# Two more down rounds per layer by seven block products, and the weight sums of the gate and up units made by accumulating transfers

## The chip, the cores and the metric

The kernel runs on one core of a Trainium2 chip. The metric is the device time of one execution in microseconds, from runs without the profiler. The profile is of one other execution of the same program; it names the engines PE (matrix multiplication; PEld is its weight load), DVE (vector engine), ACT (scalar engine), POOL (GpSimd) and SP (the engine whose queue issues most transfers).

## The reference

Two decoder layers over 528 positions (16 learned meta tokens, then 512 tokens) with 1024 features. Each layer has a norm, an input projection, forgetting attention and retention heads side by side, an output projection, and then the part that is changed here, a gated feed-forward network of 2816 hidden features:

```
hn = rmsnorm(h, ffn_norm_g)
ff = silu(hn @ w_gate) * (hn @ w_up)      # 528 x 1024 by 1024 x 2816, twice
h  = h + ff @ w_down                      # 528 x 2816 by 2816 x 1024
```

All inputs and outputs are float32. In the second layer only the 512 real tokens are needed after the attention, since the meta tokens are dropped at the end.

## The kernel before

Features lie on the 128 partitions and tokens in the free dimension, so `h` is eight tiles of 128x528. A float32 product is made of three fast ones: each operand is split into a rounded part "hi" (written by ACT) and the rest "lo" (subtracted by DVE), and PE adds hi*hi, hi*lo and lo*hi. So each block of 128x128 weights costs three matmuls per stretch of tokens, and each weight has to be converted by ACT and DVE first (`splits`, lines L941 and L942).

The feed-forward part goes over 22 hidden tiles f of 128 features. Tiles 0 and 1 are made plainly. Each tile from 2 on is a *unit* (class `Unit`): gate and up for that f, over two halves of the input features and two halves of the tokens, are a 2x2 by 2x2 block product, and are made by seven block products instead of eight (the Strassen-Winograd scheme). That is 7 x 4 blocks x 3 = 84 matmuls of 264 tokens (256 in layer 1) instead of 96, for which sums of weights and of inputs are needed. The weight sums were made by DVE, four additions of 128x512 per unit: L1084, L1085 (`make2`), L1092 (`make3`) and L1098 (`make4`). The sums of the inputs (`x_forms`) are made once per layer, in tiles `th`/`tl`.

The down projection is done in *rounds* of hidden tiles, `ROUNDS = ((0, 2), (2, 6), (6, 10), (10, 14), (14, 18), (18, 22))`, numbered 0 to 5. A round's products are woven between those of the following round's units: each of its four units brings one pair p of output tiles (2p, 2p+1). A plain pair costs 8 weight blocks x 3 x 528 tokens: 48 matmuls of 264 in layer 0, and in layer 1 24 of 512. For rounds in `SEVENTHS` (before: 2 and 4) the pair (class `Pair`) is again a 2x2 by 2x2 block product in seven: 7 x 2 blocks x 3 = 42 matmuls of 264 (256). For it, each pair needs sums of the down weights (`make1`, `make2`, four DVE additions of 128x256, L1012, L1013, L1018, L1020) and each round needs four sums of activations, the *token forms* (`token_forms`), made by DVE and split by ACT and DVE. Form 1 is made in the third-last and fourth-last unit of its round, forms 2, 3 and 4 in the last two. Forms 2 and 3 lie in parts of the tiles `xh`/`xl` of the input (its second token half, which the units don't read in that form), and form 4 in `sqh`/`sql`, one buffer each.

Results gather in PSUM tiles: `psa` (four banks, x and keep) and `psd` (two pairs of banks); DVE adds them to `h` (L1041, L1039) or takes them into the activation (L1124 to L1139), and only then PE can use the bank again.

What sets the order: PE's instructions stand in the order that the program writes them. Those of ACT, DVE, POOL and SP are put in order by a scheduler, with priorities and a few pinned places; each engine then works off its own queue strictly in that order, and an instruction that waits holds up all behind it. Weight transfers are issued by SP (L1072 gate and up, L1006 and L1177 down) into rings: `raw` with four buffers of 512 KB, `fraw` with two. Converted weights lie in two rings, `whi`/`wlo` with two buffers and `fwhi`/`fwlo` with three. `need(j)` starts conversions three to five weight jobs ahead of their use. In the feed-forward part POOL does nothing.

## Time and profile before

| | |
|---|---|
| time, three runs | 1249.72, 1249.9 and 1250.13 us (median 1249.9) |
| the profiled execution | span 1248.2 us from the first to the last instruction; the page gives no time of its own around it, and the median lies 1.7 us above the span |
| PE busy | 1236.6 us (99%), 9387 matmuls |
| DVE busy | 1062.2 us (85%), 2033 instructions |
| ACT busy | 733.5 us (59%) |
| POOL busy | 294.6 us (24%), none of it in the feed-forward parts |
| transfers | 116.25 MB, 93 GB/s over the span |
| feed-forward part | from about 282 to 634 us (layer 0) and from about 887 to 1232 us (layer 1) |

Times in the profile are counted from the span's start. Busy time overlaps between engines. Matmuls are pipelined, so the duration of one in the profile (280 ns) is longer than the distance from one to the next; the chain of waits, which merges runs of matmuls with their count, gives that distance.

### The profile page before, as it was taken

The numbers are of one execution on the slowest core, as the hardware profiler recorded it, in microseconds if no ns is written. First come the engines' busy times: TensorE is split into PE (matmuls) and PEld (weight loads), VectorE is DVE, ScalarE is ACT, GpSimd is POOL, SyncE is SP. The second block draws the span as 40 slices with busy tenths as digits, with TensorE's granted clock in tenths as the row PEclk, the third lists the DMA queues.
The fourth block names the chain that finished last, engine by engine and source line by source line (L and its number), as shares of the span: only waits on it lengthen the run. The fifth ranks groups of instructions, "written<-read, shape, count | busy, mean of one in ns | idle before, by whom it ended". The sixth has DMA issues, their size and how long they took to land.

```text
span 1248.2 us, 24164 instructions
## 1 busy us (share of the span) xinstructions
PE 1236.6 (99%) x9387; PEld 1192.1 (96%) x9387; DVE 1062.2 (85%) x2033; ACT 733.5 (59%) x1397; POOL 294.6 (24%) x568
## 2 busy tenths in 40 slices
PE   9999999999999999999999999999999999999997
PEld 9999999999999999999999989999799999999996
DVE  7887756889997999899876877568999989998996
ACT  7767655776544555455566766567765445454554
POOL 4555655440000000000035556554400000000000
PEclk9999999999999999999999999999999999999999
DMA  6222222222433233322312222231414333333322
GB/s 238 68 77 69 78 69 85 60 85 72 133 119 102 85 102 118 103 86 85 114 65 85 63 84 75 68 94 52 141 54 135 111 102 102 100 104 102 102 69 69
DMA packets 43347, 116.25 MB, mean 93 GB/s; under 512 B 5088, under 2 KB 9952, under 8 KB 43232
## 3 DMA queue, kind: packets, MB, share of 16 engines
q1 hardware_dynamic: 42800, 114.41, 28.8%
q8 instruction: 74, 1.21, 0.4%
q14 instruction: 41, 0.34, 0.1%
q10 hardware_dynamic: 432, 0.29, 0.1%
HBM read 112.58 MB, written 2.10 MB: 92 GB/s over the span
## 4 chain that ended last, share of the span: by engine, by line
PE 90%; DVE 5%; ACT 2%; DMA 1%; issue 1%; SPq 0%; ACTq 0%; DVEq 0%
PE psd L231 28%; PE psa L953 22%; PE psd L953 15%; PE psd L1197 8%; PE psa L231 5%; PE psa L1197 3%; PE psa L452 2%; PE psa L619 2%; PE psa L549 1%; PE psa L753 1%; PE psa L789 1%; DMA raw<-w_down 1%; DVE wlo L942 1%; DVE fwlo L942 0%; PE psa L312 0%
## 5 line engine op out<-in xcount | busy, mean ns | idle before, releaser
L208 POOL TENSOR_TENSOR wlo<-raw,whi 128x128 fp32r<-128x128 f32 x488 | 254.6, 557 | 212.2 <-ACT whi L204 212.2
L231 PE MATMUL psd<-xh,whi 128*128 128x264 f32 (+1 forms) x696 | 169.7, 313 | 0.0
L231 PE MATMUL psd<-xh,wlo 128*128 128x264 f32 (+1 forms) x696 | 161.0, 301 | 0.0
L231 PE MATMUL psd<-xl,whi 128*128 128x264 f32 (+1 forms) x696 | 160.6, 300 | 0.0
L231 PEld LDWEIGHTS psd<-xh,whi 128*128 128x128 f32 x696 | 112.6, 190 | 3.3 <-ACT whi L204 0.3
L231 PEld LDWEIGHTS psd<-xh,wlo 128*128 128x128 f32 x696 | 111.1, 188 | 4.4
L231 PEld LDWEIGHTS psd<-xl,whi 128*128 128x128 f32 x696 | 111.7, 189 | 2.5
L941 ACT CAST fwhi<-raw 128x512 fp32r<-128x512 f32 (+2 forms) x88 | 66.2, 757 | 72.3 <-PE psd L953 28.7
L204 ACT CAST whi<-raw 128x512 fp32r<-128x512 f32 (+1 forms) x140 | 82.1, 612 | 32.5 <-PE psd L231 17.3
L127 POOL MEMSET kc<- 64x528 f32 x4 | 2.1, 534 | 367.5 <-PE psd L1197 367.3
L942 DVE TENSOR_TENSOR fwlo<-raw,fwhi 128x512 fp32r<-128x512 f32 (+2 forms) x88 | 75.1, 854 | 7.5 <-ACT fwhi L941 7.4
L941 ACT CAST whi<-raw 128x1024 fp32r<-128x1024 f32 (+2 forms) x72 | 56.8, 789 | 37.6 <-PE psd L953 21.1
L1117 ACT COPY e<-psa 128x264 f32<-128x264 f32 (+1 forms) x120 | 44.9, 374 | 53.5 <-PE psa L953 51.9
L953 PE MATMUL psa<-th,fwhi 128*128 128x264 f32 (+1 forms) x248 | 70.4, 284 | 0.0
L953 PE MATMUL psa<-tl,fwhi 128*128 128x264 f32 (+1 forms) x248 | 70.1, 283 | 0.0
L953 PE MATMUL psa<-th,fwlo 128*128 128x264 f32 (+1 forms) x248 | 70.1, 283 | 0.0
L953 PE MATMUL psa<-th,whi 128*128 128x264 f32 (+1 forms) x232 | 65.4, 282 | 0.0
L942 DVE TENSOR_TENSOR wlo<-raw,whi 128x1024 fp32r<-128x1024 f32 (+1 forms) x72 | 64.1, 893 | 1.5 <-ACT whi L941 1.4
L953 PE MATMUL psa<-tl,whi 128*128 128x264 f32 (+1 forms) x232 | 65.4, 282 | 0.0
L953 PE MATMUL psa<-th,wlo 128*128 128x264 f32 (+1 forms) x232 | 65.3, 281 | 0.0
L566 ACT ACTIVATE pr<-pr,nmax 128x144 f32<-128x144 f32 (+1 forms) x64 | 36.8, 575 | 45.7 <-DVE nmax L553 26.3
L941 ACT CAST fwhi<-S 128x1024 fp32r<-128x1024 f32 (+1 forms) x34 | 28.8, 846 | 34.0 <-PE psa L953 14.3
(442 smaller groups left out, 4381.7 us busy)
## 6 DMA issues: line engine op xcount, KB each, us to landing
raw<-w_in SPq DMA_DIRECT2D x54, 512.0 KB, 3.5
raw<-w_gate SPq DMA_DIRECT2D x44, 512.0 KB, 3.5
fraw<-w_up SPq DMA_DIRECT2D x40, 512.0 KB, 3.5
raw<-w_down SPq DMA_DIRECT2D x80, 256.0 KB, 3.7
raw<-w_out SPq DMA_DIRECT2D x16, 512.0 KB, 3.5
h<-x_t SPq DMA_DIRECT2D x8, 264.0 KB, 4.5
dec<-decay SPq DMA_DIRECT2D x8, 264.0 KB, 2.7
raw<-w_up SPq DMA_DIRECT2D x4, 512.0 KB, 3.9
```

Source lines behind the costliest of these rows:

```text
L204: pin(nc.scalar.copy(hi, job["raw"][:, c0:c1]), pinned)
L208: pin(sub(lo[:, c:c + step], job["raw"][:, c0 + c:c0 + c + step], hi[:, c:c + step].bitcast(F32)), pinned)
L231: nc.tensor.matmul(ps[1][b][:, 0:c1 - c0], w[:, wk, :], x[:, c0:c1], start=(k == 0 and i == 0), stop=(k == n - 1 and i == 2))
L452: nc.tensor.transpose(ps[:, 128 * j:128 * j + 128], src[:, o:o + 128], idt)
L549: nc.tensor.matmul(sc[0:nq, 0:c1 - c0], qq[:, q0:q0 + nq], kk[:, c0:c1], start=(i == 0), stop=(i == 1))
L566: nc.scalar.activation(pr, pr, AF.Exp, bias=nmax[0:nq], scale=-1.0, accum_out=rsum)
L619: nc.tensor.matmul(po[:, c0:SEQ], v[:, j, :], pp[:, j, META + c0:T], start=(j == 0 and i == 0), stop=(j == 4))
L941: nc.scalar.copy(hi, src)
L942: nc.vector.tensor_sub(lo, src, hi.bitcast(F32))
L953: nc.tensor.matmul(bank()[:, 0:b.shape[-1]], a[:, o + k, :], b, start=(fresh and k == 0 and i == 0), stop=(k == n - 1 and i == 2), skip_gr ...
L1117: nc.scalar.copy(self.t["e"][:, i], self.t["x"][:, 0:w])
L1197: nc.tensor.matmul(v[:, 0:c1 - c0], a[:, s * n + k, :], b[:, c0:c1], start=(k == 0 and i == 0), stop=(k == n - 1 and i == 2))
```

## The change

Rounds 1 to 4 are now all made by seven products, not 2 and 4 alone. Where two such rounds follow each other, the forms of the later one are to lie in the same tiles as those of the earlier one, which PE still reads; so `later_form` makes forms 2, 3 and 4 of the first chunk at places in the last unit of the round, each behind the last product of the earlier round that reads its tile.

The four weight additions per unit on DVE are gone. In their place `load_sums(f)` gathers all sums of a unit in a tile `F` of five parts of 128x512 (two buffers): SP loads up (two halves) and three copies of halves of gate; then POOL issues three transfers that add to what lies in the destination: up once more from memory onto parts 1 and 2, part 2 onto part 0, part 0 onto part 4. Each of the three waits for the one before. `load_sums(f + 1)` stands at the start of unit f. The gate tile is still loaded to `raw` for the unit's first weights. The signs of the sums differ, so `x_forms` is written with other signs, and the activation takes a factor of -RSC. The ring `fraw` and one of the two `S` buffers make room for `F`.

By the order of instructions, PE has in layer 0 48 fewer matmuls of 264; in layer 1 192 fewer of 512 and 336 more of 256. SP issues 120 more transfers, POOL 120 accumulating ones, 80 of them from SBUF to SBUF.

```
-SEVENTHS = (2, 4)
+SEVENTHS = (1, 2, 3, 4)
...
             halves[k] = halves[k], u2
+            if r - 1 not in SEVENTHS:
+                for n in (3, 2, 4):
+                    later_form(r, n, k)
+            elif k:
+                for n in (2, 3):
+                    later_form(r, n, k)
+
+        def later_form(r, n, k):
+            (a, b), (c, d) = ([t[:, i] for i in range(2)] for t in halves[k])
+            if n == 4 and k == 0:
+                forms[r] = [tt("sqh", F32R), tt("sql", F32R)]
+            o, x, y = {2: (a, d, a), 3: (b, d, b), 4: (c, c, a)}[n]
+            hi, lo = [two(t)[:, k] for t in forms[r]] if n == 4 else [two(t)[:, 1] for t in st["x"][k if n == 3 else 2 + k]]
+            with tc.high_priority() if k and n < 4 else ExitStack():
+                nc.vector.tensor_sub(o, x, y)
+                split(hi, lo, o)
+            forms[r, n, k] = hi, lo
+
+        def later_forms(r, n, *ks):
+            return [lambda k=k: later_form(r, n, k) for k in ks] if r in SEVENTHS and r - 1 in SEVENTHS else []
...
-                s = self.t["s"] = fft("S", F32, (128, HB, 128), 2)
+                s = self.t["s"] = fft("S", F32, (128, HB, 128), 1)
...
+        def load_sums(f):
+            def go():
+                if f >= NF:
+                    return
+                t = wsum[f] = fft("F", F32, (128, 5, HB, 128), 2)
+                a, b = w_gate[l, f], w_up[l, f]
+                nc.sync.dma_start(t[:, 2:4], quarters(b))
+                for i, k in ((1, 0), (0, 0), (4, HB)):
+                    nc.sync.dma_start(t[:, i], a[:, k:k + HB])
+                nc.gpsimd.dma_start(t[:, 1:3], quarters(b), accum_op=ALU.add)
+                nc.gpsimd.dma_start(t[:, 0], t[:, 2], accum_op=ALU.add)
+                nc.gpsimd.dma_start(t[:, 4], t[:, 0], accum_op=ALU.add)
+            return go
...
             def make2(self, hi, lo):
-                a, b = self.t["a"], self.t["b"]
-                s = self.t["s"] = fft("S", F32, (128, NK, 128), 2)
                 with tc.high_priority() if self.f == PLAIN else ExitStack():
-                    nc.vector.tensor_add(s[:, HB:NK], b[:, 0:HB], b[:, HB:NK])
-                    nc.vector.tensor_sub(s[:, 0:HB], s[:, HB:NK], a[:, 0:HB])
-                    splits(hi, lo, s)
+                    splits(quarters(hi), quarters(lo), wsum[self.f][:, 0:3:2])
...
             def make3(self, hi, lo):
-                a, b = self.t["a"], self.t["b"]
                 with tc.high_priority(60) if self.f == PLAIN else ExitStack():
-                    nc.vector.tensor_sub(b[:, 0:HB], a[:, 0:HB], b[:, 0:HB])
-                    splits(hi, lo, b)
+                    splits(quarters(hi), quarters(lo), wsum[self.f][:, 1:4:2])
...
             def make4(self, hi, lo):
-                a, s = self.t["a"], self.t["s"]
-                nc.vector.tensor_sub(a[:, HB:NK], a[:, HB:NK], s[:, 0:HB])
-                splits(hi, lo, a[:, HB:NK])
+                splits(hi, lo, wsum.pop(self.f)[:, 4])
...
+                if f > PLAIN:
+                    steps.append(load_sums(f + 1))
...
-                    steps += d[0] + m[:NK] + d[2] + m[NK:] + d[1] + d[3] + t[:HB] + d[4] + t[HB:] + d[5] + d[6]
+                    i = r if f == f1 - 1 else None
+                    steps += (d[0] + m[:NK] + d[2] + m[NK:] + d[1] + later_forms(i, 2, 0) + d[3] + t[:HB] + d[4]
+                              + later_forms(i, 3, 0) + t[HB:] + d[5] + d[6] + later_forms(i, 4, 0, 1))
...
+        steps.insert(20, load_sums(PLAIN + 1))
...
+        steps.insert(NK + 2, load_sums(PLAIN))
```

Here is how the change moves instructions, at three places.

SP's queue in the middle of layer 0's feed-forward part (`raw` holds a unit's gate weights or a pair's down weights). Before:

```order
L1072 DMA fraw_6052<-w_up 128x1024 [waits DMAHW4_49,DVE_49]
L1072 DMA raw_6050<-w_gate 128x1024 [waits DMAHW6_49,DMAHW7_49,DMAHW5_49,DVE_49]
L1006 DMA raw_6058<-w_down 128x512 [waits DVE_49]
L1006 DMA raw_6058<-w_down 128x512
L1072 DMA raw_6248<-w_gate 128x1024 [waits DMAHW2_49,DMAHW3_49,DMAHW0_49,DVE_49]
L1072 DMA fraw_6250<-w_up 128x1024 [waits DMAHW1_49,DVE_49]
```

Now:

```order
L1103 DMA raw_6552<-w_gate 128x1024 [waits DMAHW5_49,DVE_49,Activation_49]
L1019 DMA raw_6558<-w_down 128x512 [waits DMAHW6_49,DVE_49,Activation_49]
L1019 DMA raw_6558<-w_down 128x512 [waits DMAHW7_49]
L1079 DMA F_6456<-w_up 128x1024 [waits DMASW4_49,DMASW5_49,DMASW3_49,DMAHW0_49,DVE_49,Activation_49]
L1081 DMA F_6456<-w_gate 128x512 [waits DMAHW1_49]
L1081 DMA F_6456<-w_gate 128x512 [waits DMAHW2_49]
L1081 DMA F_6456<-w_gate 128x512 [waits DMAHW3_49]
```

A unit's four transfers became seven. The first into `F` waits for the three accumulating transfers of the unit that held the buffer two units ago (DMASW) and for ACT and DVE, which read it last.

POOL's queue where layer 0's feed-forward part begins. Before, its subtractions for the output projection were followed by the memsets of layer 1:

```order
L208 TENSOR_TENSOR rql_3940<-raw_3937,rqh_3939 128x128 [waits DMAHW2_49,DVE_49,Activation_49]
L208 TENSOR_TENSOR rql_3940<-raw_3937,rqh_3939 128x128 x3
L208 TENSOR_TENSOR rkl_3942<-raw_3937,rkh_3941 128x128 [waits DVE_49,Activation_49]
L208 TENSOR_TENSOR rkl_3942<-raw_3937,rkh_3941 128x128 x3
L127 MEMSET kc0_8550 64x528 [waits DVE_49,PE_49,Pool_49]
```

Now the accumulating transfers of units 2, 3, 4 and on stand there:

```order
L1082 DMA F_4283<-w_up 128x1024 [waits DMAHW2_49,DMAHW3_49,DVE_49,PE_49]
L1083 DMA F_4283<-F_4283 128x512 [waits DMAHW4_49,DMASW0_49]
L1082 DMA F_4414<-w_up 128x1024 [waits DMAHW7_49,DMAHW6_49,Pool_49]
L1084 DMA F_4283<-F_4283 128x512 [waits DMAHW5_49,DMASW1_49]
L1083 DMA F_4414<-F_4414 128x512 [waits DMAHW0_49,DMASW2_49]
L1084 DMA F_4414<-F_4414 128x512 [waits DMAHW1_49,DMASW4_49]
L1082 DMA F_4731<-w_up 128x1024 [waits DMAHW2_49,DMASW3_49,DMAHW3_49,DVE_49,Activation_49]
```

Each L1083 waits for its unit's L1082, and each L1084 for its L1083.

DVE's queue at the end of a round, in layer 0 (`al` is the last unit's activation; `xl1`, `xl3` and `sql` take lo parts of token forms; L1041, now L1054, adds to `h`). Before, at the end of round 2:

```order
L982 TENSOR_TENSOR tq_5517<-tq_5914,tq_5517 128x264 [waits DVE_49]
L1041 TENSOR_TENSOR h0_73<-psa_5997,h0_73 128x264 [waits PE_49]
L155 TENSOR_TENSOR al1_5919<-tq_5914,ah1_5918 128x528 [waits Activation_49]
L155 TENSOR_TENSOR xl1_4150<-tq_5517,xh1_4149 128x264 [waits Activation_49]
L982 TENSOR_TENSOR tq_5914<-tq_5914,tq_5517 128x264 [waits DVE_49]
L942 TENSOR_TENSOR wlo_6046<-raw_5838,whi_6045 128x512
L155 TENSOR_TENSOR xl3_4158<-tq_5914,xh3_4157 128x264 [waits Activation_49]
```

Now, at the end of the same round:

```order
L992 TENSOR_TENSOR tq_5609<-tq_6016,tq_5609 128x264 [waits DVE_49]
L992 TENSOR_TENSOR tq_5609<-tq_6016,tq_5609 128x264
L155 TENSOR_TENSOR al1_6021<-tq_6016,ah1_6020 128x528 [waits Activation_49]
L155 TENSOR_TENSOR xl3_4161<-tq_5609,xh3_4160 128x264 [waits Activation_49]
L155 TENSOR_TENSOR xl1_4153<-tq_5609,xh1_4152 128x264 [waits Activation_49]
L992 TENSOR_TENSOR tq_6016<-tq_6016,tq_5609 128x264 [waits DVE_49]
L944 TENSOR_TENSOR wlo_6145<-F_5833,whi_6144 128x512 [waits DMASW2_49]
```

The parts of the forms that come from the last chunk stand behind the activation as before, and the conversion of the unit's last weights, now read from `F`, stands among them. The parts from the chunk before (their subtractions and splits) stand further ahead in the same unit: before, within eight rows of each other; now spread over some twenty, each split behind the last product of round 1 that reads its tile.

More of the change, by code (lines that the diff above doesn't have):

```diff
@@ L974, in token_forms @@
                 return
-            if k == 0:
-                forms[r] = [tt("sqh", F32R), tt("sql", F32R)]
-            (a, b), (c, d) = ([t[:, i] for i in range(2)] for t in (halves.pop(k), u2))
-            four = [two(t)[:, k] for t in forms[r]]
-            second, third = ([two(t)[:, 1] for t in st["x"][i]] for i in (2 + k, k))
-            for n, o, x, y, (hi, lo) in ((3, b, d, b, third), (2, d, d, a, second), (4, c, c, d, four)):
-                with tc.high_priority() if k and n < 4 else ExitStack():
-                    nc.vector.tensor_sub(o, x, y)
-                    split(hi, lo, o)
-                forms[r, n, k] = hi, lo
+            halves[k] = halves[k], u2
+            if r - 1 not in SEVENTHS:
[7 more added lines that the diff above has]
+            if n == 4 and k == 0:
+                forms[r] = [tt("sqh", F32R), tt("sql", F32R)]
+            o, x, y = {2: (a, d, a), 3: (b, d, b), 4: (c, c, a)}[n]
[6 more added lines that the diff above has]
+            return [lambda k=k: later_form(r, n, k) for k in ks] if r in SEVENTHS and r - 1 in SEVENTHS else []
         def form(r, n):
@@ L1053, in steps, with quarters @@
                         product(self.w2, 2, form(r, 4), x, False, True, 2, self.add(1, 0, "x")))
+        wsum = {}
+        def quarters(t):
+            return t.rearrange("p (s k) c -> p s k c", s=2)
+        def load_sums(f):
[11 more added lines that the diff above has]
+            return go
         class Unit:
@@ L1069, in load @@
                 if "a" not in self.t:
-                    for n, src, pool, tag, bufs in (("a", w_gate, wp, "raw", 4), ("b", w_up, phase["ffn"], "fraw", 2)):
-                        self.t[n] = pool.tile([128, NK, 128], F32, name=tag, tag=tag, bufs=bufs)
-                        nc.sync.dma_start(self.t[n], src[l, self.f])
+                    self.t["a"] = wp.tile([128, NK, 128], F32, name="raw", tag="raw", bufs=4)
+                    nc.sync.dma_start(self.t["a"], w_gate[l, self.f])
             def make1(self, hi, lo):
@@ L1422, in ffn @@
         return steps
+    neg = const.tile([128, DEPTH * HB], F32, name="neg")
+    for i in range(DEPTH):
+        nc.vector.tensor_scalar_mul(neg[:, i * HB:i * HB + HB], vec[:, V_FFN + i * NK + HB:V_FFN + i * NK + NK], -1.0)
     gf = const.tile([128, NK], F32, name="gf")
```

22 lines of the change are left out of this document (12 added, 10 removed).

## The prediction

> **What bounds the kernel now.** I read the page first, its busy times and slices:
>
> ```profile
> PE 1236.6 (99%) x9387; PEld 1192.1 (96%) x9387; DVE 1062.2 (85%) x2033; ACT 733.5 (59%) x1397; POOL 294.6 (24%) x568
> PE   9999999999999999999999999999999999999997
> DVE  7887756889997999899876877568999989998996
> POOL 4555655440000000000035556554400000000000
> ```
>
> PE has work from end to end. Next, what PE waited for, over the whole span:
>
> ```profile
> PE psd L953 <- DVE al L155: 0.3, 1, 0.3
> PE psd L1197 <- DVE al L155: 0.2, 1, 0.2
> PE psd L1197 <- ACT ah L155: 0.2, 1, 0.2
> PE psd L953 <- ACT ah L155: 0.2, 1, 0.2
> ```
>
> In the feed-forward parts that is all, 0.9 us, and all of it for activations. Weights are never late. So time there is the number of matmuls by their distance. The stretches show who comes second (one unit with a plain pair, then one with a pair in seven; PE, PEld, DVE, ACT, POOL busy, then clock, DMA share, GB/s):
>
> ```profile
> 385.70:401.80 16.10, 16.10 (x135) 16.10 (x134) 12.57 (x21) 7.28 (x11) 0.00 (x0) 1.00 0.43 131
> 447.50:463.00 15.50, 15.50 (x130) 15.50 (x129) 15.48 (x29) 8.00 (x13) 0.00 (x0) 1.00 0.27 87
> ```
>
> With a pair in seven DVE has no room left (15.48 of 15.50 us), POOL has all of it, and the DMA engines are busy for about a third.
>
> **The matmuls, the only term on the path.** The chain of waits gives the distance of matmuls, with runs of known count (start, us, what):
>
> ```profile
> 365.64 2.92 PE psa L1197 x24
> 371.49 2.95 PE psd L1197 x24
> 984.65 2.76 PE psd L1197 x12
> 1036.63 2.13 PE psa L953 x18
> ```
>
> The first two are 264 tokens wide: 2.92/24 = 0.122 us each. The third is 512 wide in layer 1: 0.230 us. The fourth is 256 wide: 2.13/18 = 0.118 us. Two more rounds with four pairs each make eight pairs per layer. Layer 0: 8 x (48 - 42) = 48 fewer by 0.122 = 5.9 us. Layer 1: 192 of 512 go, 44.2 us; 336 of 256 come, 39.7 us; gain 4.5 us. Together **10.4 us**. With PE never waiting, this is also the most that the change can bring.
>
> **DVE.** The distance from one DVE instruction to the next, by size, from the timeline (start, us):
>
> ```profile
> 429.50 0.68 DVE L1085 TENSOR_TENSOR S<-S,raw 128x512 f32<-128x512 f32 x1
> 430.10 0.68 DVE L1092 TENSOR_TENSOR fraw<-raw,fraw 128x512 f32<-128x512 f32 x1
> 430.71 0.42 DVE L155 TENSOR_TENSOR sql<-tq,sqh 128x264 fp32r<-128x264 f32 x1
> 431.05 1.22 DVE L942 TENSOR_TENSOR fwlo<-raw,fwhi 128x1024 fp32r<-128x1024 f32 x1
> 432.19 0.42 DVE L1041 TENSOR_TENSOR h<-psa,h 128x264 f32<-128x264 f32 x1
> ```
>
> So 0.60 us for 512, 0.34 for 264, 1.14 for 1024. A unit loses its four additions of 512: 2.4 us, over 40 units 96 us. Each of 16 new pairs gets four additions of 256 (1.4 us), 14 blocks of conversion for 8 (2.1 for 1.1 us) and five adds of 264 with one of 528 for two of 528 (2.3 for 1.2 us): 3.5 us, 56 us in all. The forms of four new rounds are 14 small instructions less one wide, some 4.9 us each: 20 us. Net DVE loses about 20 us. What matters is a unit which has both a pair in seven and forms to make: 15.4 - 2.4 + 1.2 = 14.2 us of DVE beside 126 matmuls, 126 x 0.122 = 15.4 us of PE. So DVE, full before with pairs in seven, gets a tenth of room, and I cost it at nothing. ACT gets the casts to the same blocks, at most as long as the 76 us that DVE gains in them, on 733 of 1248 us; SP gets 120 issues of 0.33 us (row below). Both stay hidden under PE.
>
> **The transfers.** These are the change's unknown: the trace has no transfer issued by POOL and none that accumulates. The rows nearest to it are plain loads (KB each, us from issue to landing) and the queue's totals:
>
> ```profile
> q1 hardware_dynamic: 42800, 114.41, 28.8%
> raw<-w_gate SPq DMA_DIRECT2D x44, 512.0 KB, 3.5
> raw<-w_down SPq DMA_DIRECT2D x80, 256.0 KB, 3.7
> 455.62 0.33 SPq L1072 DMA_DIRECT2D fraw<-w_up  x1
> ```
>
> 114.41 MB in 28.8% of 1248.2 us are 318 GB/s with all sixteen engines busy, 1.65 us for 512 KB; the other 1.85 us of a load's 3.5 us is latency. The four loads of one `F` (1280 KB, 4.1 us at that rate) land in about 6.0 us. An accumulating transfer of 512 KB costs at the least what the plain load costs, 3.5 us, and at the most three passes one after the other (read source, read destination, write), 10.5 us; for 256 KB, 3.7 and 11.1 us. I take the row that it is nearest to, the plain load, plus a second read at the same rate (1.65 and 0.8 us), since two operands have to come in: 5.2 and 4.5 us. Until the unit's first sums (`make2`, behind L1083) the chain is then 6.0 + 5.2 + 4.5 = 15.7 us, between 13.2 and 27.6.
>
> The time it has: `F` has two buffers, so the chain starts when `make4` of unit f-1 has been read by DVE and must end before `make2` of f+1. In DVE's new order a unit is 27 rows long (one period, 15.4 us), and `make4` stands 14 rows behind `make2`, 8.0 us. So there are 2 x 15.4 - 8.0 = **22.8 us** for the chain: 7 us of cover. By bandwidth: a unit now moves 2304 KB plainly (7.4 us at 318 GB/s) and 1024 KB accumulating, 3.3 us at the plain price and 6.6 us at twice it: 14.0 of 15.4 us. This is tight, and it goes over at 2.4 times the plain price. I cost the transfers at nothing, with these two bounds as the points where they begin to set the pace.
>
> The Trainium skill speaks to the price. Its page "Collectives: The Full Stack" ("Part 3: Why 7x under link rate", on the bandwidth ceiling) says that a reduce in the DMA engines isn't slowed by the add but by its two source reads, and comes to about half of a copy's rate. By that rule the accumulating share is the 6.6 us that I took, and the forecast stands; no row here can show it.
>
> **Waits.** New is that ACT and DVE can wait for `F`, with conversions, PSUM adds and activations queued behind them, and SP's next weights behind its wait for DVE. At the ends of rounds, where the activation just made is needed by PE some 8 us later (24 + 6 + 24 matmuls and the last pair's end), the 0.9 us of waits quoted first come from two rounds per layer; with four I add 1.0 us.
>
> **The sum.** Span 1248.2 - 10.4 + 1.0 = 1238.8; the median of the runs lies 1.7 us above the span, so **1240.5 us**.
>
> **Rivals.**
>
> *Slow accumulation (slower).* If an accumulating transfer costs three times the plain one, the unit's transfers take 7.4 + 9.9 = 17.3 us and set the period instead of 15.4: 1.9 us x 40 = 76 us. By the chain (27.6 us against 22.8), two units take 4.8 us longer, 2.4 us each: 96 us. So about 1240.5 + 85 = 1325 us. It decides from 2.4 times the plain price, or a chain of 22.8 us. For it: nothing like it is in the trace, and loads of the next weights share the engines. Against it: a share of a third now.
>
> *POOL held by DVE (slower).* POOL has to issue its transfers beside a DVE that is never idle in those stretches. If POOL only got through when DVE stops, no sum would come while DVE works, and each unit would pay its two accumulations (5.2 + 4.5 us) in series, 9.7 us x 40: about 1630 us. For it: DVE's 15.48 of 15.50 us. Against it: before, POOL and DVE worked side by side in the attention part (slices above). The Trainium skill's page "SBUF — State Buffer" ("Summary: rules for kernel authors") advises to issue transfers under DVE work from ACT or SP, since DVE's double-rate modes starve POOL's descriptor writing; by that rule DVE's rows above (0.54 us more for 512 elements more, one element per ns) are single rate and leave POOL free.
>
> *The first sums come late.* Units 2 and 3 hold both buffers, and unit 4's `make2` stands only 14 rows behind `make4` of unit 2. Before, these stood here:
>
> ```profile
> 313.48 0.69 DVE L942 TENSOR_TENSOR fwlo<-raw,fwhi 128x512 fp32r<-128x512 f32 x1
> 324.42 1.22 DVE L942 TENSOR_TENSOR fwlo<-S,fwhi 128x1024 fp32r<-128x1024 f32 x1
> ```
>
> That is 10.2 us for a chain of 15.7: DVE would wait 5.5 us in each layer. PE needs that sum only some 16 us later (unit 3's 108 matmuls and unit 4's first 24, 16.1 us), so I charge nothing; if nothing covered it, 11 us, 1251.5 us: no change.
>
> *DVE overflows at the ends of rounds.* The last unit of a round makes all twelve instructions of forms 2 to 4: 13.0 + 4.1 = 17.1 us against 15.4. Three such ends per layer, 1.7 us each: 10 us if none is absorbed, 1250.5 us.
>
> **Chances.** The forecast 0.58; slow accumulation 0.22; POOL held 0.02; late first sums 0.08; overflow 0.10. The last two, if they come, come in part, half of their chance still faster. A measurement here tells 0.2% (2.5 us) from no change. So faster 0.58 + 0.09 = 0.67, same 0.09, slower 0.24. The forecast's own range is 1239.0 (no new wait at all is 1239.5) to 1244. For eight in ten the range takes in both partial cases and the mild end of slow accumulation: 1238.5 to 1265.
>
> **What would show it.** PE's matmuls 9479 with the distances above, and span - PE busy still about 12 us: the first term. DVE busy near 1040 us, with idle time in the stretches of rounds 2 to 4. POOL's issues with landings near 5.2 and 4.5 us, and no wait of ACT's or DVE's conversions from `F` for DMA beyond unit 4. It is wrong if PE's list of waits shows conversions (`whi`, `wlo`) with several us, if ACT or DVE wait for `F` in every unit, or if the DMA share stands near 1 in the feed-forward parts.

## The result, and the profile after

The changed kernel takes 1288.3 us (median of four runs, 1287.1 to 1295.9) against 1250.0 us before: ratio 1.032, 95% interval 1.029 to 1.034. It is slower by some 38 us, where 1240.5 us was forecast (range 1238.5 to 1265). The profiled execution took 1287.1 us, its span 1285.3 us.

From the page of the changed kernel, busy times, slices and queues, and from its answer on transfers (KB each, median us from issue to landing):

```profile
PE 1240.3 (96%) x9483; PEld 1199.7 (93%) x9483; DVE 1046.3 (81%) x2115; ACT 759.9 (59%) x1485; POOL 400.2 (31%) x688
PE   9999999999799999999999999999987999999997
DMA  6222222147888788887322222222657887888841
q1 hardware_dynamic: 60080, 145.88, 34.4%
q0 software_dynamic: 17280, 41.95, 18.9%
...
F<-w_up POOLq DMA_DIRECT2D x40, 512.0 KB, 6.4
F<-F POOLq DMA_DIRECT2D x80, 256.0 KB, 4.8
```

The PE slices dip where each layer's feed-forward part begins (slice 11, and 31 to 32). The DMA engines, at a third before, are now 0.7 to 0.9 busy in most slices of these parts. DVE has room, as forecast (1046 us busy, about 1040 forecast). PE should have been busy for 1226 us and is so for 1240. Outside its busy time there are 45.0 us instead of 11.6. What it waited for (us in total, times, longest):

```profile
PE psa L955 <- ACT e L1140: 16.5, 3, 8.5
PE psd L955 <- DVE sg L1154: 4.8, 4, 1.9
PE psa L955 <- DVE fwlo L944: 4.5, 1, 4.5
PE psa L955 <- DVE h L1054: 4.2, 2, 3.1
PE psd L955 <- DVE al L155: 3.4, 6, 0.8
```

The account of the profiled execution: matmuls saved -10.4; time outside PE's busy time +33.4 (45.0 - 11.6); busy time beyond the count of matmuls +14.1 (1240.3 - 1226.2). Sum +37.1, the difference of the spans. Of the 33.4 us, 20.7 are three stops: 8.5 us in layer 0, 4.5 and 7.6 us in layer 1. The other 12.7 us are a dozen short waits, nearly all at ends of rounds.

**The stop of 8.5 us.** Timeline of layer 0 (start us, us, engine, line; idle time before, and what ended it):

```profile
313.53 0.70 SPq L1079 DMA_DIRECT2D F<-w_up  x1
...
320.70 0.86 POOL L1082 DMA_DIRECT2D F<-w_up  x1 [11.55 <-DMA F<-w_gate]
328.79 0.88 POOL L1083 DMA_DIRECT2D F<-F  x1 [7.23 <-DMA F<-w_up]
...
332.12 1.04 ACT L943 CAST fwhi<-F 128x1024 fp32r<-128x1024 f32 x1 [9.07 <-issue]
333.07 0.37 ACT L1140 COPY e<-psa 128x264 f32<-128x264 f32 x1
...
333.49 0.59 PE L955 MATMUL psa<-th,fwhi 128*128 128x264 f32 x1 [8.49 <-ACT e L1140]
```

The buffer that unit 2 held comes free, and SP starts unit 4's chain at 313.53. Its loads, the first accumulating transfer and the second follow one another, and ACT can read the sum at 332.1, 18.6 us later (the profile names no releaser in that row, but POOL's next transfer, at 332.44, waited for the same landing). PE doesn't need that sum yet. But in ACT's queue its conversion (332.12) stands ahead of a copy of unit 3 (333.07), for which PE waits. The product that it copies had ended at about 323.5, so the copy could have been made some 9 us before. The stop of 7.6 us in layer 1 has the same rows.

**The stop of 4.5 us** in layer 1 is one more of this kind, a little earlier:

```profile
936.13 0.62 ACT L943 CAST fwhi<-F 128x512 fp32r<-128x512 f32 x1 [5.14 <-DMA F<-F]
936.66 0.61 ACT L155 CAST ah<-tq 128x512 fp32r<-128x512 f32 x1
...
941.24 1.22 DVE L944 TENSOR_TENSOR fwlo<-raw,fwhi 128x1024 fp32r<-128x1024 f32 x1
...
942.52 0.58 PE L955 MATMUL psa<-xh,fwlo 128*128 128x256 f32 x1 [4.52 <-DVE fwlo L944]
```

ACT waits 5.1 us for the sums of unit 2's last weights, which PE needs much later. Behind that stands the activation of hidden tile 1, DVE waits for it, and so converts unit 3's first weights late.

**The slow clock.** Stretches of 4 us around the first stop (PE, PEld, DVE, ACT, POOL busy, then granted clock, DMA share, GB/s):

```profile
328.00:332.00 4.00, 0.00 (x0) 0.00 (x0) 0.00 (x0) 0.00 (x0) 0.88 (x1) 0.50 0.72 190
332.00:336.00 4.00, 2.51 (x11) 2.51 (x12) 2.81 (x4) 2.96 (x5) 1.76 (x2) 0.50 0.51 77
336.00:340.00 4.00, 4.00 (x29) 4.00 (x28) 2.40 (x7) 0.86 (x3) 0.07 (x1) 0.79 0.99 239
```

The granted clock falls to 0.50 during the stop and stays there for some 4 us after PE goes on (29 matmuls in 4 us, where 33 are usual). Against the usual distances of the same matmuls, those behind each of the four stops over 3 us (the three above and one of 3.1 us below) took 1.6 to 2.9 us longer while the clock was 0.50, 8.7 us in all. So each of the three costs 2 to 3 us more than it lasts. The other 5.4 of the 14.1 us lie in the refilling of PE after waits and in small differences elsewhere; they were not split further.

**The end of a round**, layer 0. First the timeline, then the last stretch of 4 us before it:

```profile
406.60 0.33 SPq L1079 DMA_DIRECT2D F<-w_up  x1
...
422.95 0.86 POOL L1083 DMA_DIRECT2D F<-F  x1 [7.42 <-DMA F<-w_up]
...
424.46 1.12 SPq L1019 DMA_DIRECT2D raw<-w_down  x1
...
431.26 1.04 ACT L943 CAST fwhi<-F 128x1024 fp32r<-128x1024 f32 x1 [4.34 <-DMA F<-F]
...
432.50 0.42 DVE L1025 TENSOR_TENSOR S<-raw 128x256 f32<-128x256 f32 x1 [3.80 <-DMA raw<-w_down]
...
433.32 0.59 PE L955 MATMUL psa<-sqh,whi 128*128 128x264 f32 x1 [3.12 <-DVE h L1054]
```

```profile
428.00:432.00 4.00, 2.21 (x19) 2.00 (x17) 0.70 (x2) 0.74 (x1) 0.52 (x1) 1.00 0.99 342
```

The DMA engines are full (0.99). Two transfers are late in it: the second accumulating one of a unit (422.95), which ACT gets at 431.26, 24.7 us after its chain began, and a down load of 256 KB issued at about 425, which DVE gets at 432.50. In DVE's queue the addition to `h`, which frees PE's bank, stands behind the sum of that load. So this stop was ended by the down load; the other stop for `h`, of 1.1 us, has the same rows. In layer 1 the longest stops at the ends of rounds stand behind the chain:

```profile
1066.07 1.05 ACT L943 CAST fwhi<-F 128x1024 fp32r<-128x1024 f32 x1 [4.15 <-DMA F<-F]
...
1067.15 1.22 DVE L944 TENSOR_TENSOR fwlo<-F,fwhi 128x1024 fp32r<-128x1024 f32 x1 [3.70 <-ACT fwhi L943]
...
1069.03 0.39 PE L955 MATMUL psd<-xh,whi 128*128 128x256 f32 x1 [1.81 <-DVE sg L1154]
```

DVE's step for `sg` stands behind its part of the conversion. In the steady part of layer 1 ACT waited for `F` as follows (stretch from 980 to 1250 us):

```profile
ACT fwhi L943 <- DMA F<-F: 13.7, 6, 4.3
ACT whi L943 <- DMA F<-F: 9.5, 6, 4.3
```

So the first theory was ORDER: late first sums, paid because ACT works in order. Its rivals were TRANSFERS (full DMA engines make everything late) and FORMS (DVE overflows at the ends of the added rounds).

### The profile page after: what moved, and what is told of

Its sections match the earlier page's. It is cut to its first block, busy times and chain, and to the rows that moved or that the text cites. A ratio compares the mean times of both kernels' runs of the same rounds, so it can differ in the third digit from the quotient of the medians.

```text
span 1285.3 us, 25152 instructions
## 1 busy us (share of the span) xinstructions
PE 1240.3 (96%) x9483; PEld 1199.7 (93%) x9483; DVE 1046.3 (81%) x2115; ACT 759.9 (59%) x1485; POOL 400.2 (31%) x688
## 3 DMA queue, kind: packets, MB, share of 16 engines
q1 hardware_dynamic: 60080, 145.88, 34.4%
q0 software_dynamic: 17280, 41.95, 18.9%
q8 instruction: 74, 1.21, 0.4%
## 4 chain that ended last, share of the span: by engine, by line
PE 60%; DVE 17%; DMA 11%; issue 7%; ACT 3%; SPq 1%; POOL 1%; ACTq 0%; DVEq 0%; POOLq 0%
PE psd L231 22%; PE psa L955 15%; PE psd L955 10%; DMA F<-F 4%; DMA F<-w_gate 3%; PE psa L231 3%; DVE fwlo L944 2%; PE psa L452 2%; DVE wlo L944 2%; PE psa L619 2%; PE psa L549 1%; PE psd L1220 1%; PE psa L753 1%; DMA F<-w_up 1%; DMA raw<-w_down 1%
## 5 line engine op out<-in xcount | busy, mean ns | idle before, releaser
L1083 POOL DMA_DIRECT2D F<-F x40 | 34.8, 869 | 231.0 <-DMA F<-w_up 216.0
L943 ACT CAST fwhi<-F 128x1024 fp32r<-128x1024 f32 (+1 forms) x62 | 55.6, 897 | 84.0 <-DMA F<-F 36.8
L1084 POOL DMA_DIRECT2D F<-F x40 | 34.7, 868 | 180.3 <-DMA F<-F 167.6
L943 ACT CAST fwhi<-raw 128x512 fp32r<-128x512 f32 (+2 forms) x90 | 61.1, 695 | 48.8 <-PE psd L955 42.0
L944 DVE TENSOR_TENSOR fwlo<-F,fwhi 128x1024 fp32r<-128x1024 f32 (+1 forms) x62 | 63.8, 1030 | 28.4 <-ACT fwhi L943 28.2
L1082 POOL DMA_DIRECT2D F<-w_up x40 | 37.0, 924 | 153.1 <-DMA F<-w_gate 57.8
L943 ACT CAST whi<-F 128x1024 fp32r<-128x1024 f32 (+1 forms) x58 | 53.1, 916 | 41.2 <-PE psa L955 14.5
L944 DVE TENSOR_TENSOR fwlo<-raw,fwhi 128x512 fp32r<-128x512 f32 (+2 forms) x90 | 70.4, 782 | 6.3 <-ACT fwhi L943 4.2
L944 DVE TENSOR_TENSOR wlo<-F,whi 128x1024 fp32r<-128x1024 f32 (+1 forms) x58 | 61.1, 1054 | 12.2 <-ACT whi L943 11.9
```

Source lines behind the costliest of these rows:

```text
L943: nc.scalar.copy(hi, src)
L944: nc.vector.tensor_sub(lo, src, hi.bitcast(F32))
L1082: nc.gpsimd.dma_start(t[:, 1:3], quarters(b), accum_op=ALU.add)
L1083: nc.gpsimd.dma_start(t[:, 0], t[:, 2], accum_op=ALU.add)
L1084: nc.gpsimd.dma_start(t[:, 4], t[:, 0], accum_op=ALU.add)
```

## The experiments

### One half of the change at a time

```
 # from the changed kernel
-SEVENTHS = (1, 2, 3, 4)
+SEVENTHS = (2, 4)
```

> Only the sums by accumulating transfers; the down rounds as before (2 and 4 by seven). Three theories of the changed kernel's loss. ORDER: the first sums of each layer come late and ACT, which works in order, holds unit 3's copies and unit 1's activation behind the conversions that wait for them; PE stood 8.5 + 4.5 + 7.6 = 20.7 us for that, and ran at a granted clock of 0.5 for some us after each stop (about 10 us more). TRANSFERS: the DMA engines are near full in the whole feed-forward part, loads land in 6 to 8 us instead of 3.5, and small waits arise everywhere. FORMS: DVE overflows at the ends of the two added rounds (12.4 us of PE waits there). Here PE's work is again that of before. ORDER: 1250 + 20.7 + 10 = about 1281 us, with the same three stops. If FORMS is right for the rest: no waits at ends of rounds, 1281. If TRANSFERS is right for the rest: these waits (12.4 us) stay, about 1290.

Measured: 1330.3 us, ratio 1.064 (1.063 to 1.066). None of the theories had said that. The copies again:

```profile
PE psa L955 <- ACT e L1140: 53.5, 8, 10.1
```

Eight stops for a copy (1.4 to 10.1 us) instead of two long ones, four per layer, most of them in units that carry a plain pair. The mechanism of ORDER is there, but it isn't bound to a layer's start: it strikes wherever the sums' conversion stands ahead of a copy while the chain is late.

```
 # from the kernel before: later_form and its places as in the change, and
-SEVENTHS = (2, 4)
+SEVENTHS = (1, 2, 3, 4)
```

> Only the two added rounds by seven; DVE makes the weight sums as before, and nothing accumulates. PE's work falls by 10.4 us, to about 1226. ORDER and TRANSFERS: no stop at a layer's start, full clock, landings near 3.5 us. DVE has 2.4 us more per unit than in the changed kernel: in a unit with a pair in seven and forms 14.2 + 2.4 = 16.6 of 15.4 us, in eight more units of each layer, and it has 76 us more than before (about 1138). FORMS: with DVE over its room by 1 to 4 us in some eight units it must be slower than 1240 (10.4 us gained), by 8 to 20 us: 1248 to 1260. If DVE had room enough: 1240.

Measured: 1313.4 us, ratio 1.051 (1.049 to 1.052), so worse than even FORMS had it. PE waits for conversions, and those for DVE's sums of down weights, which DVE, now busy for 1136 us, makes late (the first row is PE's, the second ACT's):

```profile
PE psa L953 <- ACT fwhi L941: 34.5, 8, 6.1
...
ACT fwhi L941 <- DVE S L1024: 52.5, 21, 5.5
```

Without relief for DVE the added rounds cost 63 us. Each half alone is worse than both together: the rounds need the relief, and the relief by transfers costs.

### Taking the accumulating transfers away

```
-                nc.gpsimd.dma_start(t[:, 1:3], quarters(b), accum_op=ALU.add)
-                nc.gpsimd.dma_start(t[:, 0], t[:, 2], accum_op=ALU.add)
-                nc.gpsimd.dma_start(t[:, 4], t[:, 0], accum_op=ALU.add)
```

> The changed kernel without its 120 accumulating transfers; F keeps what SP loads, so the units' sums are left out and the products are of the single halves. All conversions and products stay. The chain to a unit's sums is then one of loads, about 6 us instead of 18.6, and 42 of 190 MB go. ORDER: all three stops go (20.7 + 10 us): about 1257 us, waits at ends of rounds (12.4 us) stay if they are DVE's (FORMS). TRANSFERS: these go too, about 1242 to 1245 us.

Measured: 1241.6 us, ratio 0.993 (0.992 to 0.995). This is the forecast of the changed kernel within 1.1 us:

```profile
PE 1227.6 (99%) x9483; PEld 1190.5 (96%) x9483; DVE 1046.7 (84%) x2115; ACT 762.0 (61%) x1485; POOL 294.7 (24%) x568
...
PE psd L955 <- DVE al L155: 1.2, 2, 0.6
```

With all 16 pairs, all forms and all conversions in place, PE waits some 2 us in the feed-forward parts. FORMS falls for the changed kernel: relieved of the sums, DVE doesn't overflow at the ends of rounds. The whole loss, 1288.3 - 1241.6 = 46.7 us, is the accumulating transfers'.

```
-                nc.gpsimd.dma_start(..., accum_op=ALU.add)    # all three
+                nc.gpsimd.dma_start(...)
```

> The changed kernel with the 120 transfers of POOL as plain copies of the same bytes between the same places, in the same chain; the additions are left out. If it is the price of adding in flight (the second read): a copy of 256 KB lands in about 3.7 us or less and one of 512 KB in 3.5, the chain to the first sums shrinks from 18.6 to some 13 us and the pressure on the engines falls by a third of the accumulating share: 1255 to 1265 us. If it is the chain itself (three transfers in series behind four loads) whatever they do: 1275 to 1288 us.

Measured: 1261.9 us, ratio 1.009 (1.008 to 1.011), as the price of adding in flight had it.

```profile
q0 software_dynamic: 12160, 41.95, 9.3%
...
F<-w_up POOLq DMA_DIRECT2D x40, 512.0 KB, 4.1
F<-F POOLq DMA_DIRECT2D x80, 256.0 KB, 2.6
...
PE psa L955 <- ACT e L1140: 11.4, 2, 6.0
```

The same 41.95 MB take 9.3% of 1260.3 us as copies, 358 GB/s, and 18.9% of 1285.3 us as additions, 173 GB/s: adding costs 2.07 times the engine time. It accounts for 26.4 of the 46.7 us; the other 20.3 us are paid for three transfers in series even when they only copy, above all in two stops at the layers' starts (11.4 us).

### Start and steady part

ORDER's own test moves one conversion on ACT:

```
+                        st["kept"] = nc.scalar.copy(self.t["e"][:, i], self.t["x"][:, 0:w]).ins
...
-                with tc.high_priority() if self.f == PLAIN else ExitStack():
+                with tc.high_priority() if self.f == PLAIN else tc.issue_after(st["kept"]) if self.f == PLAIN + 2 else ExitStack():
                     splits(quarters(hi), quarters(lo), wsum[self.f][:, 0:3:2])
```

> The changed kernel with one edit of order: in each layer ACT's conversion of unit 4's first sums is queued behind unit 3's copies instead of ahead of them. No transfer changes. ORDER: the stops of 8.5 and 7.6 us and the slow clock after them go (16.1 + some 5 us), PE needs that conversion only some 16 us later: 1288 - 21 = about 1267 us; the stop of 4.5 us in layer 1 stays. TRANSFERS: PE waits about as long for the weights themselves a little later: 1280 to 1288 us.

Measured: 1283.5 us (1274.5 to 1289.1). The two stops for the copy are gone from the profile, as ORDER had it, but only some 5 us came back, as TRANSFERS had it:

```profile
PE psd L955 <- DVE sg L1154: 14.7, 7, 4.5
...
334.00 1.04 ACT L943 CAST fwhi<-F 128x1024 fp32r<-128x1024 f32 x1 [7.13 <-DMA F<-F]
```

The chain isn't earlier: ACT gets this sum at 334.0, not at 332.1. Behind unit 3's copies it still waits 7.1 us, DVE waits for it to make its part of the conversion, and behind that stands the step (`sg`) for which PE waits next. A late operand in a strictly ordered queue finds another victim.

To split the loss without moving any work, the accumulating transfers were left out in units 2 to 4 of each layer, or issued in these alone:

```
+                if f < PLAIN + 3:      # in the other run: f >= PLAIN + 3
+                    return
                 nc.gpsimd.dma_start(t[:, 1:3], quarters(b), accum_op=ALU.add)
```

> The changed kernel without the accumulating transfers of units 2, 3 and 4 of each layer (their sums are left out); all else, the order of the conversions and the other 34 units' transfers too, stays. It splits the 46.7 us between 1241.6 (no accumulating transfer at all) and 1288.3. START: the three stops of 20.7 us at the layers' starts and the slow clock after them go: about 1288 - 29 = 1259 us, the waits at the ends of rounds stay. STEADY: if the loss is mostly in the steady part and the start only moves it: 1275 us or more.

> The opposite: accumulating transfers in units 2, 3 and 4 of each layer alone (sums of the others left out). START: 1241.6 + 29 = about 1270 us. STEADY: below 1255 us. If the two shares add up, the run without the first and this one lie together 46.7 us above twice 1241.6.

Measured: 1262.8 us without those of the start, 1271.4 us with these alone (1257.8 to 1267.4; 1269.4 to 1272.4). Both are START's numbers within 4 us. Waits of PE, in this order:

```profile
PE psd L955 <- DVE sg L1156: 8.0, 7, 2.1
```

```profile
PE psa L955 <- ACT e L1142: 16.0, 2, 8.4
PE psa L955 <- DVE fwlo L944: 5.2, 1, 5.2
```

The start costs 25.5 us (1288.3 - 1262.8) or 29.8 us (1271.4 - 1241.6), the steady part 21.2 or 16.9 us. Together these exceed the whole loss by 4 us, less than the 9.6 us by which the runs of the kernel without the start's transfers scatter, so the shares add up as far as these runs can tell. In the second run the three stops stand where they stood in the changed kernel (7.7, 5.2 and 8.4 us), with the DMA engines at 0.4 to 0.5 in most slices afterwards: six chains of 40 make for some 60% of the loss.

```
-                    splits(quarters(hi), quarters(lo), wsum[self.f][:, 0:3:2])
+                    splits(hi, lo, self.t["a"])      # make2; make3 and make4 likewise
```

> The changed kernel with all loads into F and all 120 accumulating transfers, but nothing reads F: the units convert the gate tile again in place of the sums, so the sums are left out of the computation. The traffic is that of the changed kernel (190 MB); what is gone is that ACT and DVE wait for the chain. Without the accumulating transfers the time was 1241.6 us, with them 1288. CHAIN (conversions wait for a chain of 18 to 20 us, and in order of their queue hold up what PE needs): about 1242 to 1246 us. TRANSFERS (full DMA engines make the plain loads of gate and down weights late): 1260 to 1288 us, with waits for loads of raw.

Measured: 1417.2 us, which neither theory allows, and it answers another question. With no reader, the scheduler put `F`'s loads ahead on SP's queue, and the weights that are read stood behind them, while the gate tiles were held longer:

```profile
SPq L1079 <- DMA F<-F: 341.5, 41, 15.5
...
DVE S L1025 <- DMA raw<-w_down: 136.0, 13, 29.1
```

So the run doesn't tell traffic from chain. It shows that SP's queue too pays for a wait on the chain.

### Other ways to the sums

All of these make every sum.

```
-                nc.vector.tensor_add(s[:, HB:NK], b[:, 0:HB], b[:, HB:NK])
+                nc.gpsimd.tensor_add(s[:, HB:NK], b[:, 0:HB], b[:, HB:NK])   # and the three others
```

> The two added rounds with the four additions of a unit as computation on POOL, from the same two loads of 512 KB as before the change; no F, nothing accumulates, 116 MB. POOL has nothing else there; it took 0.56 us for a subtraction of 128x128 before, so about 2.2 us for one of 128x512, 8.9 us of a unit's 15.4, and 4.4 us from the loads to the first sums. If late sums and traffic were the whole loss: PE 1226 us and about 12 us beside it, 1240 to 1244 us, faster than before. If POOL's additions slow DVE or come late too: 1255 to 1300 us.

Measured: 1337.4 us, ratio 1.070 (1.068 to 1.071). Timeline of DVE and POOL in layer 0:

```profile
406.57 2.33 DVE L942 TENSOR_TENSOR wlo<-fraw,whi 128x1024 fp32r<-128x1024 f32 x1
...
407.78 2.26 POOL L1103 TENSOR_TENSOR fraw<-raw,fraw 128x512 f32<-128x512 f32 x1
...
414.79 1.21 DVE L942 TENSOR_TENSOR fwlo<-raw,fwhi 128x1024 fp32r<-128x1024 f32 x1
```

A subtraction of 128x1024 takes DVE 1.21 us alone and 2.33 us while POOL adds. DVE's busy time came to 1157 us instead of the 1046 of the same work without POOL's additions, more than the 1136 us of the run in which DVE made all four sums itself.

A middle way lets one accumulating transfer per unit stand (up onto two parts of `F`, now three parts of 256 KB) and keeps the other sums in the gate tile:

```
+                t = wsum[f] = fft("F", F32, (128, 3, HB, 128), 3)
...
+                nc.gpsimd.dma_start(t[:, 0:2], quarters(b), accum_op=ALU.add)
...
+                    nc.vector.tensor_add(a[:, 0:HB], t[:, 0], t[:, 2])              # third sum
...
+                nc.vector.tensor_add(a[:, HB:NK], a[:, HB:NK], a[:, 0:HB])          # fourth sum
```

> The changed kernel with one accumulating transfer per unit instead of three (up onto two parts of F); DVE adds the other two sums into the gate tile, which it holds anyway. F has three parts and three buffers, and each F is loaded a unit earlier. The chain to the first sums is 5 + 6.3 + 0.6 = 12 us instead of 18.6 to 20, it may begin a unit (15.4 us) earlier, and the traffic falls to 1792 KB plain and 512 KB accumulating per unit. DVE has 1.3 us more per unit, 1098 us in all, 15.5 us in a unit with a pair in seven and forms. If late first sums and full DMA engines were the loss: no stops at a layer's start, landings near 4 us, PE 1226 and some 15 us beside it: 1241 to 1246 us, faster than before. If DVE has no room for 1.3 us (it had none at 2.4 us more, 1313 us): waits of PE for DVE at the ends of rounds, 1250 to 1275 us.

Measured: 1278.4 us, ratio 1.022 (1.021 to 1.024): the second case of the expectation, a little above its range.

> As the run with three buffers, but F has two buffers and is loaded as late as in the changed kernel; the same traffic and the same DVE work. It tells the room that the chain has from the traffic. If the room decides: at a layer's start the chain of 12 us has some 10 us, stops of 2 to 3 us in each layer with their slow clock, so 6 to 10 us slower than with three buffers. If traffic decided the loss: no difference.

Measured: 1274.3 us, not slower than with three buffers. So `F`'s lead didn't decide here. Both show the same line, DVE late with conversions: three of the four waits are at ends of rounds, and the longest is at layer 1's start, where DVE has worked without a gap for 17 us by then:

```profile
PE psa L955 <- DVE fwlo L944: 13.0, 4, 4.1
```

> As the run with three buffers, but the fourth sum is added by a second accumulating transfer (256 KB in SBUF, onto the gate tile, issued after the third sum is there) instead of DVE: DVE has 0.66 us more per unit than the changed kernel, 1072 us; the transfer has some 8 us until its conversion and lands in about 4.5. If DVE's room decides between the two: some 5 to 15 us faster than the run with three buffers, 1240 to 1246 us. If accumulating transfers on the way to a conversion cost wherever they stand: slower than it.

(The fourth sum's line becomes `nc.gpsimd.dma_start(a[:, HB:NK], a[:, 0:HB], accum_op=ALU.add)`, issued behind the third sum.) Measured: 1266.3 us, ratio 1.013 (1.011 to 1.014). Taking 23 us of additions off DVE (1092.4 to 1069.0 us busy) brought 12 us, as expected, but not the 1246. It is the fastest of the kernels with four rounds that make all sums, 22 us better than the change, and still slower than the kernel before.

> Three buffers of three parts as in the run with a second accumulating transfer, but DVE makes no sum at all: the third sum too is added by a transfer of 256 KB onto the gate tile, after the unit's first weights are converted. DVE has the changed kernel's load (1046 us), F has its lead of a unit, traffic 1792 KB plain and 1024 KB accumulating. If DVE's room decides: below the 1266 us of that run by some 10 us, 1250 to 1258. If a chain that conversions wait for costs more than DVE's additions (two transfers of 4 to 5 us in series now stand behind the first conversion): 1270 to 1290 us.

(Here the third sum's line becomes an accumulating transfer too.) Measured: 1346.5 us, ratio 1.075 (1.073 to 1.077), far beyond the second case. What ACT waited for:

```profile
ACT whi L943 <- DMA raw<-F: 66.4, 17, 4.8
ACT fwhi L943 <- DMA raw<-F: 65.6, 18, 6.5
```

This chain can't start before the unit's first weights are converted, and so is late in nearly every unit (35 waits in 40 units): here 0.6 us on DVE is far cheaper than a transfer that conversions wait for.

The last two use the transfers only in some units; in the others DVE makes the sums in `F`:

```
+SUMS = range(6, 18)          # in the second: SUMS = range(6, 10), SEVENTHS = (1, 2, 4)
...
+                if f not in SUMS:
+                    nc.sync.dma_start(t[:, 1:4:2], quarters(b))
+                    return
...
+                    if self.f not in SUMS:
+                        nc.vector.tensor_add(t[:, 2], t[:, 1], t[:, 3])
+                        nc.vector.tensor_add(t[:, 0], t[:, 2], a[:, 0:HB])
```

> The changed kernel, but only units 6 to 17 (those with a pair in seven and forms at once) get their sums from the accumulating transfers; in units 2 to 5 and 18 to 21 DVE makes them as before, into F, from one load of up. The first accumulating chain then ends long before its unit. If the stops at the layers' starts are the chain's lateness: they go, with the slow clock behind them (20.7 + some 9 us), the waits at the ends of rounds stay (about 13 us with their clock): 1288 - 30 = about 1257 us. If the traffic in the steady part were the larger share of the loss: 1270 to 1280 us.

> As the run before it, but only one round more than before by seven (1, 2 and 4), so that pair and forms meet only in units 6 to 9, and only these eight units of the 40 get accumulating transfers. PE gains half of 10.4 us; DVE's load elsewhere is that of the kernel before. 1250 - 5 + 1 to 3 us for waits in units 6 to 9: 1246 to 1248 us, faster than both kernels. If a single group of such units costs as much as it brings: 1250 us or more.

Measured: 1280.4 us (1275.9 to 1287.9) and 1270.1 us (1267.4 to 1272.6). Both missed. In the first the stops for copies at the layers' starts are gone, but DVE, loaded again, waits and is late in units 2 to 5 and 18 to 21 (waits of PE for `wlo`, `fwlo` and `whi` of 1 to 4 us each). In the second PE waits for the same conversions at layer 1's start (3.3 us) and in the units behind those with transfers (1.2 to 2.0 us each).

The kernel before ran the same units without a wait, with other tiles and another order of the instructions. What part of it is the order was not tried. No kernel that makes all its sums beat the one before.

## Why the prediction was wrong

**The sum without the transfers was right.** Matmuls: 9483, as the forecast's own counts give (9387 - 48 - 192 + 336; the 9479 among its signs is a slip); -10.4 us forecast, PE's busy time fell by 9.0 us in the run without accumulating transfers, which took 1241.6 against 1240.5. DVE: 1040 forecast, 1046. Waits at the ends of rounds: +1.0 us forecast, 2 us in that run. Without the transfers the working held in each term.

**The price of a transfer was nearly right.** 5.2 and 4.5 us to landing were taken, 6.4 and 4.8 measured; twice the plain engine time was taken, 2.07 times measured. By the queues' rates (145.88 MB in 34.4% of the span are 330 GB/s) a unit's transfers take 7.1 + 6.1 = 13.2 us of engine time, where 14.0 of 15.4 were reckoned. The Trainium skill's page "Collectives: The Full Stack" ("Part 3: Why 7x under link rate") gives half a copy's rate for a reduce in the DMA engines; this case's 173 against 358 GB/s agrees. So the rival *slow accumulation* did not come by its price: the point of 2.4 times was not reached. Its other point, a chain above 22.8 us, was passed at one end of a round at least (24.7 us, below). POOL was not held by DVE: its issues took 0.87 to 0.92 us on average.

**The step that failed is the rival that was priced at nothing: the first sums come late.** Its window of 10.2 us was about right (from 313.5 to 323.0, where ACT's idle time begins, 9.5 us), its chain a little short: 15.7 us taken, 18.6 measured. Then the prediction said that "PE needs that sum only some 16 us later" and charged nothing. That is true of the sum and doesn't matter: ACT needs it when its turn comes, and what PE needs at once, a copy, stands behind it on ACT. The paragraph on waits had said that activations would be queued behind conversions; it was not carried into the price. The upper case, "if nothing covered it, 11 us", was short as well: there were three stops, not two, of 8.5, 7.6 and 4.5 us, and a slow clock behind each, which the forecast had no term for. The experiments give 25.5 to 29.8 us for them.

**The second failure is the cover of 7 us in the steady part**, by which the transfers were costed at nothing. It was reckoned with one chain of 15.7 us at the typical landings. At the end of a round above it took 24.7 us, over the cover of 22.8: its transfers shared full engines with the next unit's loads (7.42 us waited for the first accumulating transfer, some 8 us to the landing of the second, where the medians are 6.4 and 4.8), and POOL, which also works in order, stood before the previous unit's last transfer meanwhile. So 13.2 of 15.4 us, called "tight" and costed at nothing, held on the average only. PE paid for it in layer 0 behind plain down loads that came late (4.2 us in two stops for `h`) and in layer 1 mostly behind the chain (4.8 us in four stops for `sg`). Queues in strict order pay for the worst landings. The whole steady part cost 17 to 21 us.

**DVE overflow at the ends of rounds** was the right place and the wrong cause: with the same DVE work and no accumulating transfers PE waited some 2 us.

**What was open and stays so:** how much of the steady 17 to 21 us is the engines being full and how much the chain itself; the run meant for it was upset by SP's order. With plain copies in the same chain PE's stops away from the layers' starts came to 3.4 us instead of 12.7, so three transfers in series cost little there by themselves; but copies make the chain shorter and the engines emptier at once. And whether the four rounds could gain with a hand-made order of ACT and DVE in the first units was tried only in the one place.

## What to carry to other kernels

A wait isn't priced by when the operand is needed, but by what stands behind the waiting instruction on its engine: read the queue's next rows, and ask which of them someone waits for now. Moving work from a full engine to transfers is no gain if conversions then wait for a chain of them: a run that leaves the transfers out tells what the move could bring at most (here 8 us), and runs that keep them in a few units alone tell where they cost. A chain of transfers under nearly full DMA engines (0.8 and more here) has to be covered at its worst landings, not at the median.

## What the runs showed of the hardware

**Adding in flight** costs twice a copy's engine time (173 against 358 GB/s for the same bytes), and some 2.2 us more to landing (6.4 against 4.1 us for 512 KB, 4.8 against 2.6 us for 256 KB within SBUF). The smaller packets of the additions (17280 against 12160) are not the reason: in the trace a packet of 4 KB takes 366 ns on average when it adds and 182 ns when it copies. The landings also hold the fuller engines: with accumulating transfers at the layers' starts alone, 256 KB within SBUF landed in 3.3 us (median of twelve).

**Times scatter with accumulating transfers in the steady part.** Runs of the kernel before lay within 0.15%, of the one without accumulating transfers within 0.06%; with them in the steady part the runs of one kernel spread by up to 1.1% (1274.5 to 1289.1 us). That full engines are the reason is not shown: the kernel in which nothing reads `F` had shares of 0.8 to 0.9 and a spread of 0.4%.

**Short stops cost clock.** In each of the 17 traces the changes of the granted clock lie whole multiples of 3.413 us apart (in the changed kernel's at 327.475, 337.715, 433.288 and 436.702 us, among others). What counts is how long PE stands within one such step. Of the 5885 steps between 20 and 1235 us that began at 1.00, none in which PE stood for less than 1.4 us was followed by 0.50, and every one in which it stood for 1.9 us or more was. So a stop of 1.8 us within one step brought the clock to 0.50 for 3.4 us (the run without the start's transfers). One of 1.8 us in the changed kernel, and one of 3.05 us in the kernel that took 1346.5 us, each shared by two steps, left it at 1.00. The Trainium skill's page "TensorE: Matmul & The Clock Gate" ("What's actually happening") gives half the clock after an idle window of about 3.4 us that runs free of the kernel. The steps of 3.413 us and the unlike outcomes at like lengths agree with a free-running window; that some 1.9 us of standing within it are enough is less than the page says.

**POOL's arithmetic holds DVE up.** 1.21 against 2.33 us for one DVE subtraction. The Trainium skill's page "SBUF — State Buffer" ("Who interferes with whom") says that a DVE instruction with two operands in SBUF contends with a GpSimd instruction that reads SBUF; this trace agrees. POOL's transfers did no such thing: in the changed kernel the 31 subtractions of this size that ran beside an issue of POOL kept their 1.22 to 1.23 us.
